# Loads, low parts, softplus and fills moved in a hybrid decoder layer on one core

## The chip, the cores and the metric

The kernel runs on one core of one Trainium2 chip. The core has five engines that the text names by what they are: TensorE (PE in the rows: matmuls; PEld is its weight load), VectorE (DVE), ScalarE (ACT), GpSimd (POOL) and SyncE (SP), which here issues every DMA. The metric is the device time of one execution in microseconds, lower is better. Each engine works through its own list of instructions in order and waits on semaphores for the others.

## The reference

One layer of a Hymba-like decoder over 1040 tokens (16 meta tokens and 1024 of the input) of width 1024. A state-space mixer and a stick-breaking attention read the same projection, their outputs go through one output projection, and a feed-forward block with a short convolution follows.

```python
xn = rms_norm(h, mix_pre_g[l])
proj = xn @ w_in[l]                      # z | x,B,C | dt | q | k | v
...
y_ssd = ssd_mixer(z, xbc, dt_raw, ...)   # conv (4 taps) + silu, softplus(dt), chunked scan, gate with silu(z), norm
y_sb = rms_norm(stick_breaking_attention(q, k, v).reshape(Bsz, L, SB_WIDTH), sb_norm_g[l])
mix = jnp.concatenate([y_ssd, y_sb], axis=-1) @ w_out[l]
h = h + rms_norm(mix, mix_post_g[l])
...                                      # feed-forward: up, conv (3 taps), gelu, gate, down
return h[:, N_META:]
```

In the mixer, chunks of 128 tokens are worked on one after another for two groups of heads; within a chunk `y = y_diag + y_off`, then `y + xs * d_skip`, times `silu(z)`. In the attention, weights are running products of `1 - beta` over the keys.

## The kernel before

Every float32 operand of a matmul is split in a high part (a rounded copy, made by ScalarE) and a low part (the rest, one subtraction on VectorE or GpSimd), and a product takes three matmuls: high by high, high by low, low by high. Names ending in `h`/`hi` and `l`/`lo` are these parts: `wr_B` is a raw weight block, `wh_B` and `wl_B` its parts (`split_hi`, `split_lo`); `whi1z`, `wlo1z`, `wlo4z` and so on are those of weight blocks and of sums of blocks, 128 x 1024 each; `ahz` and `alz` (128 x 512) are the parts of one half of a block, made by `split_22`.

**The head.** The token tiles `xt` are loaded, squared on ScalarE (`square`), scaled with the row weights `gpre` on VectorE (`norm`, tile `xn`), transposed on TensorE (`turn_x`, tile `xtp`) and cut into parts by ScalarE and VectorE. `t1` to `t4` are sums of such tiles for the products below. The code of the head stands in a manual schedule: its instructions run on each engine in the order in which they are written.

**Products.** A `Duo` multiplies a pair of weight blocks with all tokens by seven products (Strassen's form; `product(n)`, line 308 of the matmuls) that go to three groups of PSUM banks `dA`, `dX`, `dY`. After a product VectorE adds its bank to the raw outcome in SBUF (`craw_x<-dXx`, line 320; ScalarE copies two of the seven, line 317), and the next product that uses the bank waits for that. Between the products of one duo the splits and sums of the next one are issued (`n.split_22`, `n.sums`: the sums are lines 285 to 288 on GpSimd), and in seven slots the conv taps (`conv_acts`: four taps on VectorE, lines 505 and 508, on 128 x 1040) and the softplus of dt (`dt_acts`: `loads` with the tiny `fold` and the memset of `dtk`, `turn_dt`, `soft_a`, `soft_b`, `decay`).

**What sets the order there.** From line 614 a schedule holds the order of PE, DVE, ACT and POOL as it is written, up to what the tile framework puts ahead by its own priorities; the lists that result are shown below.

**The scan.** 18 units (two groups by nine chunks). `load_zx` loads the gate `zk` and the skip term `xd`, 128 x 4 x 128 float32 each; `chunk_outputs` makes the scaled carried state `yt` (line 1116); `chunk_store` multiplies the chunk (`yt<-em,xdt`, line 1136), fills with products of q and k (`scan_fill`), adds `yt` by transposes (line 1141), and then VectorE adds `xd` (line 1145, which frees the PSUM bank for the next unit's line 1136) and multiplies by `zk` (line 1146). SyncE's list is part of the order here. The DMAs take eight completion semaphores (DMAHW0 to DMAHW7) in turn, so that a DMA is issued when the one eight places ahead of it has landed.

**The entry of attention.** `hold` is a 128 x 1040 bfloat16 mask for the scans over keys (`pair_weights`, line 1314): zero, with ones in the last 128 columns that an `affine_select` on GpSimd cuts to a triangle. `token_rstd` makes the norm of the mixer's output; its tile `tmsa` has a column that is set to one.

Of the kernel before, what the change touches and what calls it, by code (L numbers as in the profile page):

```python
# [17 lines left out]
P = 128  # L18
# [48 lines left out]
def tile_layer(ctx: ExitStack, tc: tile.TileContext, x, meta, rows, parts,  # L67
# [190 lines left out]
    class Duo:  # L258
# [14 lines left out]
        def split_22(self):  # L273
            h, l = (weight_rows(sa.tile([P, 5 * P], F32R, tag=f"a22{e}", name=f"a{e}{self.nm}", bufs=2), 4, OFF22)
                    for e in "hl")
            raw = self.r[1][:, HI4]
            nc.scalar.activation(h, raw, AF.Copy)
            nc.gpsimd.tensor_tensor(l, raw, h.bitcast(F32), op=ALU.subtract)
            self.w["a22"] = h, l
# [44 lines left out]
    with tc.tile_pool(name="pre", bufs=3, side="right") as pre:  # L324
# [14 lines left out]
        raws = {"B0": raw_of("B0", w_xbc[8])}  # L339
        gpre = row_bcast(pre, 0, D, "gpre")  # L340
        load_x(2)
        load_x(3)
# [83 lines left out]
        split_hi("B0")  # L426
        split_lo("B0")
        square(2)
        root(2)
        norm(2)  # L430
        turn_x(0)
        square(3)
# [192 lines left out]
    def dt_acts():  # L625
# [30 lines left out]
        def soft_a():  # L656
            dtx = box["dtx"]
            e, s, s2 = box["e"], box["s"], box["s2"] = [t3(n) for n in ("e1", "s1", "s2")]
            nc.vector.scalar_tensor_tensor(e, dtx, -1.0, dtx, op0=ALU.mult, op1=ALU.min)
            nc.scalar.activation(e, e, AF.Exp)  # L660
            nc.vector.tensor_scalar(s, e, 2.0, None, op0=ALU.add)
            nc.vector.reciprocal(s, s)
            nc.vector.tensor_tensor(s, s, e, op=ALU.mult)
            nc.vector.tensor_tensor(s2, s, s, op=ALU.mult)
# [42 lines left out]
        return [[loads], [turn_dt], [soft_a], [soft_b], [lambda: decay(0)], [lambda: decay(1)],  # L707
# [39 lines left out]
    for i, q in enumerate(duos):  # L747
# [3 lines left out]
        for j, m in enumerate((1, 5, 2, 6, 7, 3, 4) if i == 0 else (1, 6, 5, 7, 2, 3, 4)):  # L751
            q.product(m)
            if i == 0:
                if m == 1:
                    d0.split_4()
                elif m == 6:
                    split_t(t4l.bitcast(F32), xo["t4"], nc.vector)
            if n is not None:
                if m == 1:
                    n.split_22()  # L760
                elif m == 6:
                    n.sums()
                elif m == 7:
                    n.split_3()
                elif m == 2:
                    n.split_1()
                elif m == 3:
                    n.split_4()
            elif m in (7, 2):
                v_split(1, int(m == 2))  # L770
            for act in slots[j]:
                act()
# [4 lines left out]
        if i == 1:  # L777
            slots = merged(slots, [[], dts[2], [], dts[3], [], [], []]) + [dts[4], dts[5], dts[6]]
# [199 lines left out]
    def token_rstd(r, pool, nm, pt, scalar=False):  # L978
# [6 lines left out]
        (nc.gpsimd if scalar else nc.vector).memset(ms[:, 0:1], 1.0)  # L985
# [14 lines left out]
    with tc.tile_pool(name="ssd", bufs=1, side="right") as sp:  # L1000
# [49 lines left out]
        def load_zx(g, c):  # L1050
            a, b = (M0, NM) if c == 0 else (NM + (c - 1) * P, NM + c * P)
            y0 = M0 if c == 0 else 0
            zx = []
            for t, d in (("zk", zd), ("xd", xdd)):
                zx.append(sp.tile([P, 4, P], F32, tag=t, name=f"{t}{g}_{c}", bufs=3 if t == "zk" else 2))
                nc.sync.dma_start(out=zx[-1][:, :, y0:y0 + b - a], in_=d[g][:, :, a:b].rearrange("b p t -> p b t"))
            zxs[g, c] = zx
# [129 lines left out]
        load_zx(*units[0])  # L1187
# [4 lines left out]
        for n, (g, c) in enumerate(units):  # L1192
# [6 lines left out]
            if n + 3 < len(units):  # L1199
                load_bc(*units[n + 3])  # L1200
            if n < 2:
# [3 lines left out]
            if n + 1 < len(units):  # L1205
                load_zx(*units[n + 1])
# [62 lines left out]
    nc.vector.memset(hold, 0.0)  # L1269
    nc.vector.memset(hold[:, L - P:], 1.0)  # L1270
# [1225 lines left out]
```

## Time and profile before

| | |
|---|---|
| time, median of 3 runs | 1657.96 us (1655.59 to 1659.79) |
| the profiled execution: time | 1657.8 us |
| its span in the trace | 1655.8 us |
| mean granted clock of TensorE | 0.997 of full speed |
| TensorE busy | 1626.7 us, 98% |
| VectorE / ScalarE / GpSimd busy | 1087.5 / 748.1 / 782.1 us |
| DMA queue of SyncE | 244.48 MB, 45.8% of 16 engines |

The rows further down are those of the profiled execution. Its time is longer than its span by 2.0 us, which lie around the span. A time in a row is counted from the start of the span, and an instruction's duration includes what it spends held up after its start.

### The profile page before, as it was taken

The numbers are of one execution on the slowest core, as the hardware profiler recorded it, in microseconds if no ns is written. First come the engines' busy times: TensorE is split into PE (matmuls) and PEld (weight loads), VectorE is DVE, ScalarE is ACT, GpSimd is POOL, SyncE is SP. The second block draws the span as 40 slices with busy tenths as digits, with TensorE's granted clock in tenths as the row PEclk, the third lists the DMA queues.
The fourth block names the chain that finished last, engine by engine and source line by source line (L and its number), as shares of the span: only waits on it lengthen the run. The fifth ranks groups of instructions, "written<-read, shape, count | busy, mean of one in ns | idle before, by whom it ended". The sixth has DMA issues, their size and how long they took to land.

```text
span 1655.8 us, 28995 instructions
## 1 busy us (share of the span) xinstructions
PE 1626.7 (98%) x11508; PEld 1434.1 (87%) x11508; DVE 1087.5 (66%) x1248; ACT 748.1 (45%) x1100; POOL 782.1 (47%) x579
## 2 busy tenths in 40 slices
PE   7999999999999999999999999999999999999998
PEld 6999999978877888888877889999999999888886
DVE  6975744344367599999840677765666556658877
ACT  7454344332234367766741445433333333344544
POOL 2876877520457463454421113777777677200001
PEclk9999999999999999999999999999999999999999
DMA  4544335334588776545254542222333322495345
GB/s 173 185 154 133 104 121 194 135 138 145 148 236 266 212 235 207 155 123 154 60 193 151 165 161 90 96 96 96 98 107 113 108 98 83 142 332 175 96 119 180
DMA packets 164518, 247.39 MB, mean 149 GB/s; under 512 B 18487, under 2 KB 99495, under 8 KB 162702
## 3 DMA queue, kind: packets, MB, share of 16 engines
q1 hardware_dynamic: 163806, 244.48, 45.8%
q8 instruction: 91, 1.49, 0.4%
q10 hardware_dynamic: 576, 1.05, 0.2%
q14 instruction: 45, 0.37, 0.1%
HBM read 161.99 MB, written 83.46 MB: 148 GB/s over the span
## 4 chain that ended last, share of the span: by engine, by line
PE 89%; DVE 5%; issue 2%; POOL 2%; DMA 2%; ACT 1%; POOLq 0%; DVEq 0%; SPq 0%; ACTq 0%
PE fX L1900 10%; PE mo L1504 10%; PE dnA L2312 7%; PE fY L1900 7%; PE fA L1900 7%; PE dnB L2312 5%; PE av L1352 3%; PE tw L1332 3%; PE z L1308 3%; PE pj_q L218 3%; DVE kp L1314 2%; PE pj_k L218 2%; PE dXz L308 2%; PE dXqk L308 2%; PE dXx L308 2%
## 5 line engine op out<-in xcount | busy, mean ns | idle before, releaser
L1314 DVE TENSOR_TENSOR_SCAN kp<-kp,hold 128x396 f32<-128x396 f32 (+5 forms) x224 | 211.2, 1014 | 20.2 <-ACT kp L1309 18.4
L182 POOL TENSOR_TENSOR wlo<-wr,whi 128x1024 fp32r<-128x1024 f32 x43 | 99.3, 2318 | 40.8 <-ACT whi L181 40.8
L2349 POOL TENSOR_TENSOR fms<-fms 128x1 f32<-128x1 f32 x8 | 2.3, 288 | 222.0 <-DMA ar<-fda 185.9
L181 ACT ACTIVATE whi<-wr 128x1024 fp32r<-128x1024 f32 x43 | 45.7, 1063 | 112.2 <-PE fX L1900 76.2
L1972 DVE SCALAR_TENSOR_TENSOR ga<-gr,pp,ga 128x1024 f32<-128x1024 f32 x44 | 69.4, 1577 | 34.1 <-ACT ga L1965 33.3
L2234 ACT ACTIVATE dh<-ar 128x512 fp32r<-128x512 f32 x77 | 48.6, 631 | 94.1 <-PE dnB L2312 44.7
L2235 DVE TENSOR_TENSOR dl<-ar,dh 128x512 fp32r<-128x512 f32 x77 | 53.2, 691 | 47.1 <-ACT dh L2234 47.1
L1309 ACT ACTIVATE kp<-z 128x788 f32<-128x788 f32 (+4 forms) x96 | 72.7, 832 | 16.6 <-PE z L1308 12.4
L1337 ACT ACTIVATE th<-tw 128x1024 f32<-128x1024 f32 (+2 forms) x96 | 70.8, 813 | 15.6 <-PE tw L1332 15.6
L1352 PE MATMUL av<-th,v 128*64 128x128 f32 x1152 | 70.0, 275 | 2.0 <-POOL tmsa L985 0.9
L1332 PE MATMUL tw<-ident,kp 128*128 128x128 f32 x576 | 70.0, 276 | 0.8 <-ACT st L935 0.5
L1332 PEld LDWEIGHTS tw<-ident,kp 128*128 128x128 f32 x576 | 62.4, 141 | 8.0 <-issue 6.5
L1352 PEld LDWEIGHTS av<-th,v 128*64 128x64 f32 x1152 | 62.3, 137 | 8.0 <-issue 3.9
L2312 PE MATMUL dnA<-dl,dh 128*128 128x512 f32 x176 | 68.5, 389 | 0.0
L2312 PE MATMUL dnA<-dh 128*128 128x512 f32 x176 | 68.5, 389 | 0.0
L2312 PE MATMUL dnA<-dh,dl 128*128 128x512 f32 x176 | 68.5, 389 | 0.0
L1286 POOL TENSOR_SCALAR cb<-kp 128x32 f32<-128x32 f32 x64 | 42.9, 678 | 50.5 <-DVE kp L1314 46.9
L2033 POOL TENSOR_TENSOR al<-wr,ah 128x512 fp32r<-128x512 f32 x20 | 28.6, 1430 | 77.6 <-ACT ah L2032 77.5
L1308 PE MATMUL z<-k,q 64*128 64x396 f32 (+9 forms) x672 | 62.3, 329 | 1.0 <-DVE st L941 1.0
L1308 PEld LDWEIGHTS z<-k,q 64*128 64x128 f32 x672 | 53.1, 185 | 10.8 <-ACT th L1337 4.2
L2312 PE MATMUL dnB<-dh 128*128 128x512 f32 x132 | 51.3, 389 | 0.0
L2312 PE MATMUL dnB<-dh,dl 128*128 128x512 f32 x132 | 51.3, 389 | 0.0
(987 smaller groups left out, 6026.4 us busy)
## 6 DMA issues: line engine op xcount, KB each, us to landing
wr<-in_w_up SPq DMA_DIRECT2D x44, 512.0 KB
fds<-ga SPq DMA_DIRECT2D x44, 256.0 KB
b<-in_w_down SPq DMA_DIRECT2D x44, 256.0 KB
ar<-fds SPq DMA_DIRECT2D x44, 256.0 KB
fda<-ga SPq DMA_DIRECT2D x33, 256.0 KB
ar<-fda SPq DMA_DIRECT2D x33, 256.0 KB
k<-qkd SPq DMA_DIRECT2D x8, 1040.0 KB
q<-qkd SPq DMA_DIRECT2D x64, 128.0 KB
```

What stands on the lines that cost most here:

```text
L182: nc.gpsimd.tensor_tensor(l, raw, h.bitcast(F32), op=ALU.subtract)
L218: mm(acc[:, :CQ - s], a[:, k, :], b[:, k % 4, c + s:c + CQ], start=(k == 0 and j == 0), stop=(k == KB - 1 and j == 2))
L308: mm(acc[:, c, :CQ], u[:, k, :], v[:, k, c * CQ:(c + 1) * CQ], start=first and k == 0 and j == 0, stop=k == 3 and j == 2, skip_group_check ...
L1308: mm(z[:, j, a - lo:e - lo], u[h, :], r[h, a - bases[x]:e - bases[x]], start=s_ == 0, stop=s_ == 2)
L1309: nc.scalar.activation(kp[:, :, lo:top], z[:, :, :top - lo], AF.Sigmoid, scale=-QSCALE)
L1314: nc.vector.tensor_tensor_scan(part, part, hold[:, L - last + a:L - last + e][:, ::-1], 1.0 if e == last else kp[:, j, e:e + 1], op0=ALU.m ...
L1332: nc.tensor.transpose(tw[:, j, b, :], kp[:, j, c0:c0 + P], ident)
L1337: copied[0] = nc.scalar.activation(th[:, :, :nb, :], tw[:, :, :nb, :], AF.Copy, scale=-1.0, bias=1.0).ins
L1352: mm(av[halves[j], 1 - x, :], v[:, kb, halves[j]], th[:, j, b, :], start=kb == 0, stop=kb == i)
L1504: recent[0] = mm(acc, u[:, k, :], v[:, cs], start=(k == 0 and j == 0), stop=(k == 7 and j == 2))
L1900: mm(acc[:, c, :nn], u[:, k, :], v[:, k, c0:c0 + nn], start=first and k == 0 and j == 0, stop=k == 3 and j == 2, skip_group_check=not first)
L2312: mm(banks[BANK[n], t], u[:, 0, c], v[:, 1, :], start=(n in (1, 2, 5) and p == 0 and i == 0), stop=(p == NPR - 1 and i == 2), skip_group_c ...
```

## The change

In the head, the load of `gpre` and that of the third token tile go ahead of the load of `wr_B`, and the split of `wr_B` goes behind the third tile's square (high part) and the first tile's transposes (low part). The first duo's successor gets its `alz` on VectorE instead of GpSimd. The middle of the softplus becomes a step of its own (`soft_m`), one slot later, and its last part moves with it. In the scan, `load_zx` loads `xd` first and `zk` second, and the unit's state loads and pending stores are issued between the two. At the entry of attention the two fills of `hold` go from VectorE to GpSimd, and the column of `tmsa` is a ScalarE copy instead of a GpSimd memset.

```diff
@@ -270,12 +270,12 @@
         def split_1(self):
             self.w["a11"], self.w["a12"] = split_w(self.r[0], f"1{self.nm}")
 
-        def split_22(self):
+        def split_22(self, eng=nc.gpsimd):
             h, l = (weight_rows(sa.tile([P, 5 * P], F32R, tag=f"a22{e}", name=f"a{e}{self.nm}", bufs=2), 4, OFF22)
                     for e in "hl")
             raw = self.r[1][:, HI4]
             nc.scalar.activation(h, raw, AF.Copy)
-            nc.gpsimd.tensor_tensor(l, raw, h.bitcast(F32), op=ALU.subtract)
+            eng.tensor_tensor(l, raw, h.bitcast(F32), op=ALU.subtract)
             self.w["a22"] = h, l
 
         def sums(self):
@@ -336,9 +336,9 @@
 
         load_x(0)
         load_x(1)
-        raws = {"B0": raw_of("B0", w_xbc[8])}
         gpre = row_bcast(pre, 0, D, "gpre")
         load_x(2)
+        raws = {"B0": raw_of("B0", w_xbc[8])}
         load_x(3)
         raw_dt = pre.tile([P, KB, 16], F32, tag="wdt", name="wr_dt", bufs=1)
         nc.sync.dma_start(out=raw_dt, in_=w_dt)
@@ -423,12 +423,12 @@
             root(i)
         norm(0)
         norm(1)
-        split_hi("B0")
-        split_lo("B0")
         square(2)
         root(2)
         norm(2)
+        split_hi("B0")
         turn_x(0)
+        split_lo("B0")
         square(3)
         root(3)
         norm(3)
@@ -658,6 +658,9 @@
             e, s, s2 = box["e"], box["s"], box["s2"] = [t3(n) for n in ("e1", "s1", "s2")]
             nc.vector.scalar_tensor_tensor(e, dtx, -1.0, dtx, op0=ALU.mult, op1=ALU.min)
             nc.scalar.activation(e, e, AF.Exp)
+
+        def soft_m():
+            e, s, s2 = box["e"], box["s"], box["s2"]
             nc.vector.tensor_scalar(s, e, 2.0, None, op0=ALU.add)
             nc.vector.reciprocal(s, s)
             nc.vector.tensor_tensor(s, s, e, op=ALU.mult)
@@ -704,7 +707,7 @@
         def store():
             nc.sync.dma_start(out=dtkd, in_=dtk)
 
-        return [[loads], [turn_dt], [soft_a], [soft_b], [lambda: decay(0)], [lambda: decay(1)],
+        return [[loads], [turn_dt], [soft_a], [soft_m], [soft_b], [lambda: decay(0)], [lambda: decay(1)],
                 [lambda: decay(2), store, turn_acs]]
 
     v_stack = ExitStack()
@@ -757,7 +760,7 @@
                     split_t(t4l.bitcast(F32), xo["t4"], nc.vector)
             if n is not None:
                 if m == 1:
-                    n.split_22()
+                    n.split_22(nc.gpsimd if i else nc.vector)
                 elif m == 6:
                     n.sums()
                 elif m == 7:
@@ -775,7 +778,7 @@
         for k, acts_ in enumerate(extra):
             slots[k] = acts_ + slots[k]
         if i == 1:
-            slots = merged(slots, [[], dts[2], [], dts[3], [], [], []]) + [dts[4], dts[5], dts[6]]
+            slots = merged(slots, [[], dts[2], dts[3], [], dts[4], [], []]) + [dts[5], dts[6], dts[7]]
         if i == n_early:
             t_stack.close()
             vl = v_stack.enter_context(tc.tile_pool(name="vl", bufs=1, side="left"))
@@ -982,7 +985,10 @@
             a, nr = (M0, 2) if t == 0 else (NM + (t - 1) * P, P)
             mm(pt[:nr, t:t + 1], sq[:, a:a + nr], ones[:, 0:1], start=True, stop=True)
         ms = pool.tile([P, NT + 1], F32, tag="tms", name=f"tms{nm}")
-        (nc.gpsimd if scalar else nc.vector).memset(ms[:, 0:1], 1.0)
+        if scalar:
+            nc.scalar.activation(ms[:, 0:1], ones[:, 0:1], AF.Copy)
+        else:
+            nc.vector.memset(ms[:, 0:1], 1.0)
         for rows_, cols_ in ((slice(0, 2), slice(0, 1)), (slice(0, P), slice(1, NT + 1))):
             if scalar:
                 nc.scalar.activation(ms[rows_, cols_], pt[rows_, cols_], AF.Copy, scale=1.0 / D, bias=EPS)
@@ -1051,9 +1057,10 @@
             a, b = (M0, NM) if c == 0 else (NM + (c - 1) * P, NM + c * P)
             y0 = M0 if c == 0 else 0
             zx = []
-            for t, d in (("zk", zd), ("xd", xdd)):
-                zx.append(sp.tile([P, 4, P], F32, tag=t, name=f"{t}{g}_{c}", bufs=3 if t == "zk" else 2))
-                nc.sync.dma_start(out=zx[-1][:, :, y0:y0 + b - a], in_=d[g][:, :, a:b].rearrange("b p t -> p b t"))
+            for t, d in (("xd", xdd), ("zk", zd)):
+                zx.insert(0, sp.tile([P, 4, P], F32, tag=t, name=f"{t}{g}_{c}", bufs=3 if t == "zk" else 2))
+                nc.sync.dma_start(out=zx[0][:, :, y0:y0 + b - a], in_=d[g][:, :, a:b].rearrange("b p t -> p b t"))
+                yield
             zxs[g, c] = zx
 
         def chunk_weights(g, c):
@@ -1184,7 +1191,7 @@
         put_stores()
         set_rows(2)
         load_bc(*units[2])
-        load_zx(*units[0])
+        run(load_zx(*units[0]), 3)
         cur = chunk_weights(*units[0])
         chunk_mask(*units[0], *cur)
         run(fill, 16 - FIRST)
@@ -1198,12 +1205,13 @@
                 load_x(*units[n + 2])
             if n + 3 < len(units):
                 load_bc(*units[n + 3])
+            zx_steps = load_zx(*units[n + 1]) if n + 1 < len(units) else iter(())
+            run(zx_steps, 1)
             if n < 2:
                 put_stores()
             if n in (0, 2, 6, 10):
                 load_state(n // 2 + 2, n // 2 + (4 if n else 3))
-            if n + 1 < len(units):
-                load_zx(*units[n + 1])
+            run(zx_steps, 2)
             nxt = chunk_weights(*units[n + 1]) if n + 1 < len(units) else None
             yt, zk, xd, prev[g] = chunk_outputs(g, c, *cur)
             if nxt:
@@ -1266,8 +1274,8 @@
     ap = apool.enter_context(tc.tile_pool(name="attn", bufs=1, side="right"))
 
     hold = ap.tile([P, L], BF16, name="hold", tag="hold")
-    nc.vector.memset(hold, 0.0)
-    nc.vector.memset(hold[:, L - P:], 1.0)
+    nc.gpsimd.memset(hold, 0.0)
+    nc.gpsimd.memset(hold[:, L - P:], 1.0)
     nc.gpsimd.affine_select(out=hold[:, L - P:], in_=hold[:, L - P:], compare_op=ALU.is_ge, fill=0.0, base=0,
                             pattern=[[1, P]], channel_multiplier=-1)
```

VectorE's list from the low part of `t2` on, in the stretch of the first duo's products (`cdB` are the conv taps, `dYx` and `dXx` PSUM banks of the duo), before:

```order
L255 TENSOR_TENSOR t2l<-t2r,t2h 128x2080
L505 TENSOR_SCALAR cdB_851<-craw_B_256,pp 128x1040
L508 SCALAR_TENSOR_TENSOR cdB_851<-craw_B_256,pp,cdB_851 128x1040
L636 TENSOR_TENSOR fold<-ident 32x16
L255 TENSOR_TENSOR t3l<-t3r,t3h 128x2080
L320 TENSOR_TENSOR craw_x_838<-dYx_867,craw_x_838 128x520
L508 SCALAR_TENSOR_TENSOR cdB_851<-craw_B_256,pp,cdB_851 128x1040 x2
L320 TENSOR_TENSOR craw_x_840<-dXx_926,craw_x_838 128x520
```

And of the change:

```order
L255 TENSOR_TENSOR t2l<-t2r,t2h 128x2080
L255 TENSOR_TENSOR t3l<-t3r,t3h 128x2080
L278 TENSOR_TENSOR alz_848<-wrz_802,ahz_847 128x4x128
L505 TENSOR_SCALAR cdB_851<-craw_B_256,pp 128x1040
L508 SCALAR_TENSOR_TENSOR cdB_851<-craw_B_256,pp,cdB_851 128x1040
L636 TENSOR_TENSOR fold<-ident 32x16
L320 TENSOR_TENSOR craw_x_838<-dYx_867,craw_x_838 128x520
L508 SCALAR_TENSOR_TENSOR cdB_851<-craw_B_256,pp,cdB_851 128x1040 x2
L320 TENSOR_TENSOR craw_x_840<-dXx_926,craw_x_838 128x520
```

`t3l` moved ahead of the first two taps and `alz` came in behind it; `fold`, the evacuations of `dYx` and `dXx` and the last two taps stand behind all of them.

SyncE's list in the scan, from a table load (`sg`) to the loads of the fourth unit's `zk` and `xd` (`bt`, `ct`, `bn` are state loads), with what each waits for, before:

```order
L1040 DMA sg_4472<-diagd_808 8x1024 [waits DMAHW3_49]
L1014 DMA bt_4461<-bcd_596 128x256 [waits DMAHW4_49]
L1015 DMA ct_4462<-bcd_597 128x256 [waits DMAHW5_49]
L1018 DMA bn_4463<-bnd_600 128x256 [waits DMAHW6_49]
L1014 DMA bt_4464<-bcd_598 128x256 [waits DMAHW7_49]
L1015 DMA ct_4465<-bcd_599 128x256 [waits DMAHW0_49]
L1018 DMA bn_4466<-bnd_601 128x256 [waits DMAHW1_49]
L1056 DMA zk_1_4847<-zd_114 128x4x128 [waits DMAHW2_49,Activation_49]
L1056 DMA xd_1_4849<-xdd_102 128x4x128 [waits DMAHW3_49,DVE_49]
```

And of the change:

```order
L1046 DMA sg_4472<-diagd_808 8x1024 [waits DMAHW3_49]
L1062 DMA xd_1_4841<-xdd_102 128x4x128 [waits DMAHW4_49,DVE_49]
L1020 DMA bt_4461<-bcd_596 128x256 [waits DMAHW5_49]
L1021 DMA ct_4462<-bcd_597 128x256 [waits DMAHW6_49]
L1024 DMA bn_4463<-bnd_600 128x256 [waits DMAHW7_49]
L1020 DMA bt_4464<-bcd_598 128x256 [waits DMAHW0_49]
L1021 DMA ct_4465<-bcd_599 128x256 [waits DMAHW1_49]
L1024 DMA bn_4466<-bnd_601 128x256 [waits DMAHW2_49]
L1062 DMA zk_1_4849<-zd_114 128x4x128 [waits DMAHW3_49,Activation_49]
```

`xd` moved from behind the six state loads and `zk` to the place ahead of them; `zk` stands where `xd` stood. Both wait for a semaphore of a landing eight places earlier.

## Rows read from the trace of the kernel before

**Rows 1.** TensorE's waits: tile waited with <- tile waited for: us, times, longest.
```profile
PE xtp L383 <- DVE xn L369: 12.1, 5, 10.2
...
PE av L1352 <- POOL tmsa L985: 0.9, 1, 0.9
```

**Rows 2.** Timeline of TensorE: start, us, instruction, [idle before <- releaser].
```profile
69.23 0.39 PE L308 MATMUL dXx<-t3h,whi3x 128*128 128x260 f32 x1 [0.96 <-DVE craw_x L320]
...
85.52 0.58 PE L308 MATMUL dXz<-t2h,wlo4z 128*128 128x260 f32 x1 [1.05 <-POOL wlo4z L182]
...
467.61 1.85 PE L1136 MATMUL yt<-em,xdt 128*64 128x128 f32 x16 [2.02 <-DVE xd L1145]
...
471.74 0.60 PE L1141 MATMUL yt<-ident,yt 128*128 128x128 f32 x4
```

**Rows 3.** Stretches: us; busy PE, PEld, DVE, ACT, POOL; PEclk, DMA share, GB/s.
```profile
69.40:72.40 3.00, 3.00 (x26) 2.98 (x27) 0.86 (x1) 2.11 (x2) 2.92 (x3) 1.00 1.03 399
85.50:88.80 3.30, 3.28 (x15) 3.28 (x16) 2.85 (x2) 0.53 (x2) 2.62 (x2) 0.50 0.77 308
467.80:471.10 3.30, 3.30 (x24) 2.97 (x22) 2.11 (x5) 0.63 (x1) 2.77 (x3) 0.50 0.90 272
```

**Rows 4.** Timeline of VectorE in the head.
```profile
8.83 2.47 DVE L369 SCALAR_TENSOR_TENSOR xn<-xt,rs_pre,gpre 16x1024 f32<-16x1024 f32 x2 [6.71 <-DMA gpre<-in_rows]
```

**Rows 5.** Timeline of ScalarE in the head.
```profile
7.18 1.06 ACT L415 ACTIVATE wh_B<-wr_B 128x1024 fp32r<-128x1024 f32 x1
...
21.60 0.38 ACT L249 ACTIVATE sq<-pj_dt 32x260 f32<-32x260 f32 x1 [0.41 <-PE pj_dt L247]
...
23.47 0.57 ACT L393 ACTIVATE b11h<-xtp 128x480 fp32r<-128x480 f32 x1 [0.45 <-PE xtp L383]
...
58.91 1.95 ACT L254 ACTIVATE t3h<-t3r 128x2080 fp32r<-128x2080 f32 x1 [3.35 <-DVE t2l L255]
...
65.35 1.06 ACT L181 ACTIVATE whi1z<-wrz 128x1024 fp32r<-128x1024 f32 x1
```

**Rows 6.** Timeline of VectorE around the first products.
```profile
58.80 0.81 DVE L505 TENSOR_SCALAR cdB<-craw_B,pp 128x1040 f32<-128x1040 f32 x1
59.65 1.30 DVE L508 SCALAR_TENSOR_TENSOR cdB<-craw_B,pp,cdB 128x1040 f32<-128x1040 f32 x1
...
60.95 2.31 DVE L255 TENSOR_TENSOR t3l<-t3r,t3h 128x2080 fp32r<-128x2080 f32 x1
...
63.79 4.77 DVE L508 SCALAR_TENSOR_TENSOR cdB<-craw_B,pp,cdB 128x1040 f32<-128x1040 f32 x2
68.49 0.69 DVE L320 TENSOR_TENSOR craw_x<-dXx,craw_x 128x520 f32<-128x520 f32 x1
```

**Rows 7.** Timeline of GpSimd in the same stretch.
```profile
62.65 2.67 POOL L182 TENSOR_TENSOR wlo4x<-s24x,whi4x 128x1024 fp32r<-128x1024 f32 x1 [5.95 <-ACT whi4x L181]
65.27 2.19 POOL L278 TENSOR_TENSOR alz<-wrz,ahz 128x512 fp32r<-128x512 f32 x1
67.41 0.70 POOL L637 MEMSET dtk<- 128x720 f32 x1
68.07 2.56 POOL L182 TENSOR_TENSOR wlo1z<-wrz,whi1z 128x1024 fp32r<-128x1024 f32 x1
...
82.29 3.18 POOL L182 TENSOR_TENSOR wlo4z<-s24z,whi4z 128x1024 fp32r<-128x1024 f32 x1
```

**Rows 8.** Timeline of SyncE in the scan (DMA issues).
```profile
456.57 0.35 SPq L1014 DMA_DIRECT2D bt<-bcd  x1
...
460.88 0.45 SPq L1056 DMA_DIRECT2D xd<-xdd  x1
```

**Rows 9.** Timeline of VectorE in the scan.
```profile
466.78 0.69 DVE L1145 TENSOR_TENSOR xd<-yt,xd 128x512 f32<-128x512 f32 x1 [5.77 <-DMA xd<-xdd]
```

**Rows 10.** Timeline of GpSimd at the entry of attention.
```profile
593.53 0.09 POOL L985 MEMSET tmsa<- 128x1 f32 x1
```

**Rows 11.** Timeline of VectorE at the entry of attention.
```profile
579.25 13.81 DVE L1314 TENSOR_TENSOR_SCAN kp<-kp,hold 128x396 f32<-128x396 f32 x14 [1.78 <-POOL hold L1271]
```

## The prediction

> **What bounds the kernel now.** The first section of the page gives TensorE 98% of the span, so time can be won or lost only where TensorE waits or runs slower. I read three views in turn. The waits of TensorE name what it stood for, in total [rows 1]: 12.1 us for the first normalized tiles `xn` (10.2 of them before its first instruction) and 0.9 for `tmsa`. TensorE's timeline shows three more [rows 2]: 0.96 us for `craw_x`, 1.05 for `wlo4z`, 2.02 in the scan for the `xd` addition. All five places are touched by the change. The table of stretches then shows what a wait can cost behind it [rows 3]: after the `wlo4z` wait and after the `xd` wait the granted clock is 0.50 for 3.3 us with TensorE busy throughout. That is the 1.2 GHz level instead of 2.4, so each stretch does half its work and costs about 1.7 us. After the 0.96 us it stayed at 1.00. Last, the timelines of the other engines give the durations. The order of TensorE's own instructions is the same in both kernels, so every term below is a wait of TensorE or a slow stretch.
>
> **a. Loads in the head: -0.75 us (-0.9 to 0).** The first `xn` waits for `gpre` until 8.83 [rows 4]; the first use of `wr_B` is at 7.18 [rows 5], so the 512 KB load of `wr_B` ahead of `gpre` puts `gpre` at most 1.6 us back, and `gpre` now takes its place. But ScalarE copies without a break behind 11.1 and shows only two waits before the head's end, 0.41 and 0.45 us [rows 5]. Those, 0.86, are what an earlier `xn` can give; I take 0.75, since `x3` is not moved forward.
>
> **b. `t3l` and `alz` ahead of the taps: +5.3 us (+2.9 to +6.6).** This term is seen in the order and not in the diff: VectorE now does `t3l`, `alz`, two taps and `fold` before it comes to the other two taps and to `craw_x<-dXx`, for which TensorE already waits 0.96 us. `t3l` cannot start before its `t3h` ends on ScalarE at 60.86 [rows 5], as it did before (60.95). So 3.4 us of work that stood ahead of `t3l` or on GpSimd now stands behind it. To that come GpSimd's turns: two taps, 1.30 each alone, take 4.77 while `wlo4x` ends and `alz` runs [rows 6, 7], so the two engines' instructions add up here. Step by step, from `wlo4x`'s end at 65.3 [rows 7], which stays: `alz` on VectorE, 0.6 (512 columns at the rate of `t3l`'s 2.31 for 2080), 65.9. First tap 0.81, second 1.30: 68.0. By then `whi1z` is there (65.35 + 1.06, [rows 5]), so `wlo1z` gets its turn; of the 2.56 in its row 0.45 lies behind a tap, so 2.1: 70.1. (`fold` and the evacuation of `dYx` go beside it.) Third tap: 71.4. The first of GpSimd's sums, half as many elements as `wlo1z`: 1.05, 72.5. Fourth tap: 73.8. `craw_x<-dXx`, 0.69: 74.5, against 69.2 now. That is +5.3. If GpSimd gets nothing in behind `wlo4x`, the evacuation of `dYx` (0.69, as its like in [rows 6]) is exposed instead and the end is 72.1: +2.9. If one more of GpSimd's sums gets in, with what it holds up some 1.3: +6.6. A gain is excluded, since even without any turn of GpSimd `alz`, two taps and `fold` have come behind `t3l`.
>
> **c. The clock behind that wait: +1.7 us (0 to 1.7).** A wait of 1.05 us was followed by 3.3 us at 0.50, one of 0.96 was not [rows 2, 3]. A wait of 6 us is nearer to the first; I take the full price.
>
> **d. The `wlo4z` wait goes: -2.7 us.** TensorE comes to `wlo4z` at 84.47 and gets it at 85.5 [rows 2, 7]. After a delay of 5.3 (or of 2.9) it comes at 89.8 (87.4), past that end. So the 1.05 us and the slow stretch behind, 1.7, are not paid a second time. The three together: 5.3 + 1.7 - 2.7 = +4.3 us (2.9 + 0 - 2.7 = +0.2, to 6.6 + 1.7 - 2.7 = +5.6). The tap chain also feeds ScalarE's silu and stores, for which TensorE waits in no row.
>
> **Softplus: nothing.** Its middle and last parts each move by one product or less. TensorE waits for none of it in the views, and products cover it; without the cover it would cost less than the chain's own few small instructions, under 1 us, which I leave in the range.
>
> **e. `xd` ahead of `zk`: -3.2 us (-3.7 to 0).** One unit of the scan waits, the fourth. Its `xd` is issued at 460.88, behind six loads and `zk`, the first of which went at 456.57 [rows 8], and the addition waits until 466.78 [rows 9], 5.9 us after the issue. In the new order `xd` takes the place at 456.57 and lands near 462.5, before TensorE comes to the next `yt` at 465.6. So 2.0 + 1.7 = 3.7 us go. `zk`, however, now stands where `xd` stood: issued about 460.9, landing 466.8. On VectorE the product with `zk` stands behind the addition, and behind that one small copy and the scaling of `yt`, which TensorE's transposes need: 466.8 + 0.7 + 0.3 + 0.7 = 468.5. TensorE gets there at 465.6 + 1.1 for `yt` + 1.4 for the twelve products between them, which took 2.3 at the half clock [rows 2]: 468.1. So about 0.45 is paid again. No other unit's addition holds TensorE in the trace, so there a place in the queue costs nothing.
>
> **f. Entry of attention: -0.7 us (-0.9 to +0.1).** `tmsa`'s memset stands on GpSimd at 593.53 [rows 10], and `av` waits 0.9 for it [rows 1]. On ScalarE it is one tiny copy ahead of its user. The `hold` memsets go to GpSimd, which clears 720 columns in 0.70 [rows 7], so 1040 in 1.0; VectorE's first scan already waits 1.78 us for `hold` [rows 11] and will start later by 0 to 1.0. I take +0.2 for it.
>
> **Sum.** -0.75 + 4.3 + 0 - 3.2 - 0.7 = -0.35 us on the profiled execution's 1657.8 us (span 1655.8 and 2.0 around it): 1657.45. The median of the runs is 0.16 above that execution, so 1657.6. Three places gain, one loses, and the two sides are about as large.
>
> **A rule that speaks against the change.** I let `fold`, 32x16, go beside `wlo1z`, since no row shows an instruction so small held back. If it is held like the taps [rows 6, 7], the evacuation of `dYx` behind it is late too and another sum gets in: the +6.6 end of b instead of 5.3, and the sum +0.95. The Trainium skill says this, on the page "SBUF — State Buffer", section "Who interferes with whom": a VectorE instruction with two SBUF inputs contends with a GpSimd instruction that reads SBUF, and the later one blocks until the first has ended. By that rule the trace agrees for the taps, 4.77 instead of 2.6 us; for `fold` no run here shows it.
>
> **The rivals.** The forecast, chance 0.55: the pieces cancel, 1657.6; alone 1655.5 to 1659.
> A, 0.27: GpSimd is not in the way behind `wlo4x` and no slow stretch follows, so b to d come to +0.2. For it speaks that GpSimd's turns hang on tenths of a microsecond; against it the 4.77 us of two taps. -0.75 + 0.2 - 3.2 - 0.7 = -4.45: 1653.5. With every gain at its end (-0.9 + 0.2 - 3.7 - 0.9 = -5.3): 1652.7.
> B, 0.10, the slower side: the scan's wait only changes its name, `zk` for `xd`. With the same wait e is 0: 1660.8. It makes the kernel slower by over 0.3% when e becomes +2.1, a wait of 4.1 us and its slow 1.7 against the 3.7 saved; for that `zk` must land 9.5 us after its issue, instead of the 5.9 of `xd`. Six loads stand ahead of it, but small ones.
> C, 0.08: `fold` is held, as worked out above: 1658.9.
>
> **How the numbers follow.** 0.3% of the time is 5.0 us, about what a measurement of this kernel can tell from no change: faster is below 1653.0, slower above 1662.9. Faster: the lower part of A (0.12) and the low edge of the forecast (0.03), 0.15. Slower: half of B (0.05) and the upper edges of the forecast and of C (0.04), 0.09. Same: 0.76. The range for 8 in 10 goes from A's middle part, 1653.0, to the upper end of b (+1.3) with e at 0 (+3.2), 1662.0.
>
> **What would show it.** Right: a wait of TensorE of 5 to 7 us for `craw_x` that ends near 74, a stretch at clock 0.50 behind it, no `wlo4z` wait, no `xd` wait at 465 and at most half a microsecond at the transposes, no `tmsa` wait. Wrong: `craw_x<-dXx` ending before 72, or a clock of 1.00 behind the wait (A); a wait of 2 us or more behind `zk` (B); a wait in attention for `hold` that was not there.

## The result and the profile after

The changed kernel takes 1660.64 us, median of 18 runs (1658.12 to 1665.1); the kernel before took 1657.99 in as many runs beside it (1655.06 to 1661.01). The ratio is 1.0019 with a 95% interval from 1.0012 to 1.0026, which is some 3 us, 2.0 to 4.3. The time lies in the range that was given, and the change is less than 0.3%; but the small difference has the other sign: forecast -0.4, measured +2.6.

TensorE's waits in the profiled execution after (tile waited with <- tile waited for: us, times, longest), against [rows 1, 2]:

```profile
PE xtp L383 <- DVE xn L369: 11.0, 5, 8.5
PE dXx L308 <- DVE craw_x L320: 7.4, 1, 7.4
...
PE pz L685 <- DVE s L678: 0.7, 1, 0.7
```

The waits for `wlo4z`, `xd` and `tmsa` are gone from the list and the first wait has become shorter, 11.0 instead of 12.1. In their place stands one wait of 7.4 us for `craw_x`, and a small new one for the softplus tile `s`. TensorE's timeline at the same instructions as in [rows 2], with the block of dt products (18 small ones in a row) and the first `pz` besides:

```profile
74.98 0.59 PE L308 MATMUL dXx<-t3h,whi3x 128*128 128x260 f32 x1 [7.41 <-DVE craw_x L320]
...
89.24 2.09 PE L649 MATMUL tpd<-fold,sq 32*16 32x16 f32 x18
...
91.61 0.28 PE L308 MATMUL dXz<-t2h,wlo4z 128*128 128x260 f32 x1
...
136.05 0.21 PE L685 MATMUL pz<-s,tri 16*16 16x16 f32 x2 [0.71 <-DVE s L678]
...
472.54 1.10 PE L1143 MATMUL yt<-em,xdt 128*64 128x128 f32 x16
...
475.11 0.60 PE L1148 MATMUL yt<-ident,yt 128*128 128x128 f32 x4
```

Since TensorE's list is the same in both kernels, the difference of the start of one instruction is the sum of all that lies ahead of it. At the wait for `craw_x` TensorE came at 74.98 - 7.41 = 67.57, before at 69.23 - 0.96 = 68.27: 0.7 ahead. Behind it the instruction started at 74.98 instead of 69.23, 5.75 late. At `wlo4z` it is 91.61 to 85.52, 6.1. At `yt` in the scan 472.54 to 467.61, 4.9, at the transposes 475.11 to 471.74, 3.4. At the last matmul the trace has +2.5, near the +2.65 of the medians, but that nearness is in part luck. The spans differ by 3.5 (1659.3 and 1655.8), because 1.0 more lies behind the last matmul here; that tail is 6.45 to 7.5 us, counted from the last matmul's start, in the executions of this case, also of kernels whose code there is the same. So most of the loss lies between 68 and 75, and the largest gain comes in the scan, where it was expected. The table of stretches shows the clock (PEclk is the third number from the right):

```profile
74.90:78.30 3.40, 3.32 (x15) 3.32 (x16) 1.04 (x2) 2.35 (x2) 1.84 (x2) 0.50 0.18 17
88.00:91.20 3.20, 3.20 (x30) 3.03 (x28) 1.40 (x3) 2.40 (x4) 0.00 (x0) 1.00 0.15 62
92.40:95.20 2.80, 2.80 (x15) 2.80 (x14) 2.76 (x2) 0.00 (x0) 2.64 (x3) 0.50 0.33 129
473.20:476.60 3.40, 3.40 (x31) 3.09 (x28) 2.76 (x7) 1.93 (x3) 2.37 (x3) 1.00 0.89 270
```

Behind the wait the clock is 0.50 until 78.3, as expected. It is 0.50 again from 92.4 to 95.2, where there was no wait at all: from 88.0 to 91.2 TensorE is busy throughout at 1.00, and what it did last there is the block of 18 products of dt, 32 x 16 each. In the kernel before the same block stands ahead of the slow stretch at 85.5, and the `wlo4z` wait of [rows 2] follows it:

```profile
81.95 2.09 PE L649 MATMUL tpd<-fold,sq 32*16 32x16 f32 x18
```

In the scan the clock stays at 1.00. VectorE and GpSimd around the wait, against [rows 6, 7]:

```profile
60.23 2.33 DVE L255 TENSOR_TENSOR t3l<-t3r,t3h 128x2080 fp32r<-128x2080 f32 x1 [2.01 <-ACT t3h L254]
62.47 2.68 DVE L278 TENSOR_TENSOR alz<-wrz,ahz 128x512 fp32r<-128x512 f32 x1
...
65.93 3.20 DVE L508 SCALAR_TENSOR_TENSOR cdB<-craw_B,pp,cdB 128x1040 f32<-128x1040 f32 x1
69.05 1.23 DVE L636 TENSOR_TENSOR fold<-ident 32x16 f32<-32x16 f32 x1
...
70.81 3.50 DVE L508 SCALAR_TENSOR_TENSOR cdB<-craw_B,pp,cdB 128x1040 f32<-128x1040 f32 x2
74.24 0.69 DVE L320 TENSOR_TENSOR craw_x<-dXx,craw_x 128x520 f32<-128x520 f32 x1
```

```profile
61.99 2.62 POOL L182 TENSOR_TENSOR wlo4x<-s24x,whi4x 128x1024 fp32r<-128x1024 f32 x1 [5.95 <-ACT whi4x L181]
64.55 0.70 POOL L637 MEMSET dtk<- 128x720 f32 x1
65.83 2.19 POOL L182 TENSOR_TENSOR wlo1z<-wrz,whi1z 128x1024 fp32r<-128x1024 f32 x1 [0.59 <-ACT whi1z L181]
67.99 2.26 POOL L285 TENSOR_TENSOR wrz<-wrz 128x512 f32<-128x512 f32 x1
70.33 2.89 POOL L286 TENSOR_TENSOR wrz<-wrz,wrz 128x512 f32<-128x512 f32 x1
```

Read the two lists together. `alz` takes 2.68 us instead of the 0.6 of its size: it is held until `wlo4x` ends at 64.6. The second tap takes 3.20 instead of 1.30 and is held until `wlo1z` ends at 68.0. `fold` takes 1.23 instead of 0.16 and is held until L285 ends at 70.25. The last two taps take 3.50 instead of 2.6, with L286 between them. GpSimd has an instruction ready at each gap, and three of its turns fit behind `wlo4x`.

In the scan, VectorE at the fourth unit:

```profile
467.71 0.69 DVE L1152 TENSOR_TENSOR xd<-yt,xd 128x512 f32<-128x512 f32 x1 [0.35 <-PE yt L1148]
472.68 0.69 DVE L1153 TENSOR_TENSOR zk<-xd,zk 128x512 f32<-128x512 f32 x1 [4.28 <-DMA zk<-zd]
...
473.62 0.68 DVE L1123 TENSOR_TENSOR yt<-yf,dtk 128x512 f32<-128x512 f32 x1
```

`xd`'s addition now waits 0.35 us for TensorE and not for a load. The product with `zk` waits 4.28 us for its load and holds the scaling of `yt` until 474.3; TensorE's transposes come at 475.1 and do not notice. At the entry of attention, VectorE:

```profile
582.37 18.19 DVE L1322 TENSOR_TENSOR_SCAN kp<-kp,hold 128x396 f32<-128x396 f32 x18 [2.26 <-POOL hold L1279]
```

GpSimd's first fill takes 0.97 us, and the first scan waits 2.26 us for `hold` instead of 1.78 [rows 11]. It starts 3.1 us later than before, where TensorE is 3.4 late, since VectorE has no fills of its own ahead of it now. TensorE shows no wait for `hold`.

In the head, TensorE's first instruction starts at 8.52 instead of 10.16. Of ScalarE's two waits in [rows 5] the 0.41 is gone; the other stands as it was:

```profile
22.82 0.57 ACT L393 ACTIVATE b11h<-xtp 128x480 fp32r<-128x480 f32 x1 [0.45 <-PE xtp L383]
```

### The profile page after: what moved, and what is told of

It is laid out like the page before. It is cut to its first block, busy times and chain, and to the rows that moved or that the text cites. A ratio compares the mean times of both kernels' runs of the same rounds, so it can differ in the third digit from the quotient of the medians.

```text
span 1659.3 us, 28998 instructions
## 1 busy us (share of the span) xinstructions
PE 1626.9 (98%) x11508; PEld 1434.7 (86%) x11508; DVE 1091.2 (66%) x1247; ACT 748.5 (45%) x1101; POOL 778.3 (47%) x579
## 3 DMA queue, kind: packets, MB, share of 16 engines
q10 hardware_dynamic: 576, 1.05, 0.2%
## 4 chain that ended last, share of the span: by engine, by line
PE 61%; DVE 2%; issue 1%; ACT 1%; DVEq 0%; POOLq 0%; ACTq 0%; POOL 0%
PE fX L1908 10%; PE mo L1512 10%; PE dnA L2320 7%; PE fY L1908 7%; PE fA L1908 7%; PE dnB L2320 5%; PE av L1360 3%; PE tw L1340 3%; PE z L1316 2%; DVE kp L1322 2%; PE g0a L1922 1%; PE x2tp L1786 0%; PE pj_q L218 0%; PE pj_k L218 0%; PE g0d L1922 0%
```

## The experiments

Each one's ratio is against the kernel before on the same chip, and 0.001 of it is 1.7 us.

**One part alone: `alz` on VectorE (e1)** (line 278 and its call, nothing else).

```diff
-                    n.split_22()
+                    n.split_22(nc.gpsimd if i else nc.vector)
```

> The kernel before with one part alone: alz on VectorE, which also puts t3l ahead of the taps. Theory 1 (fold is held up and the slow stretch behind the wlo4z wait belongs to the dt transposes ahead of it): the wait for craw_x 7.4 us as in the changed kernel, 6.4 more than before, 1.7 of slow clock behind it, 1.0 back at wlo4z, so +7.1 us against the kernel before. Theory 2 (the forecast's step: fold goes free, the slow stretch goes with the wlo4z wait): a wait of 6.3, no slow stretch near 92, +4.3 us. Rival: the wait comes from the head's moved loads and not from alz; then the wait stays at 1.0 and the time at +0.

1662.18 us, ratio 1.0035 (1.0021 to 1.0049): +5.8. TensorE's wait, then the stretch near 92:

```profile
PE dXx L308 <- DVE craw_x L320: 7.4, 1, 7.4
```

```profile
92.00:96.00 4.00, 4.00 (x36) 4.00 (x35) 3.96 (x4) 0.00 (x0) 3.84 (x3) 1.00 0.31 120
```

The wait of 7.4 comes from this part alone, so the head's loads have no share in it. The stretch near 92 stayed at 1.00 here, as theory 2 had it. But this is the same block of small products as in the changed kernel, where it fell; one execution does not decide that point. The size lies between the two expectations, and its interval, 3.5 to 8.1 us, takes in both.

This run also shows how far executions differ in the head, which e1, e10 and e11 have unchanged. The same TensorE instruction behind it, in the kernel before and then in e1:

```profile
61.68 0.39 PE L308 MATMUL dAx<-b21h,whi1x 128*128 128x260 f32 x1 [0.64 <-ACT craw_x L317]
60.20 0.40 PE L308 MATMUL dAx<-b21h,whi1x 128*128 128x260 f32 x1 [0.65 <-ACT craw_x L317]
```

e10 comes to it at 60.74, e11 at 60.26, and the changed kernel at 61.01. The four products `pj_dt<-b11h` ahead of it take 1.22 us before and 0.72 in e1: TensorE's speed goes up earlier in one execution than in the other.

**The softplus put back (e2)** in the changed kernel (the diff shows one of three places; the function `soft_m` and the slots go back with it).

```diff
-        return [[loads], [turn_dt], [soft_a], [soft_m], [soft_b], ...
+        return [[loads], [turn_dt], [soft_a], [soft_b], ...
```

> The changed kernel with the softplus steps where they were before. Theory 1 (the moved step makes TensorE wait for s at pz): that wait of 0.7 us (0.9 to 1.1 with the pause behind it) near 135 goes, -1.0 us against the changed kernel, so +1.6 to +2.0 against before. Theory 2 (the wait comes from the 7 us by which everything is late in the changed kernel, since VectorE has more to do behind it): the wait stays, 0 against the changed kernel.

1661.67 us, ratio 1.0027 (1.0015 to 1.0038): no gain. Of TensorE's waits the 7.4 us stayed and this is new:

```profile
PE dYx L308 <- DVE craw_x L320: 1.4, 1, 1.4
```

The wait at `pz` went, and one of 1.4 us for `craw_x` at `dYx` came. VectorE there:

```profile
125.08 2.18 DVE L664 TENSOR_TENSOR s<-s 128x144 f32<-128x144 f32 x1
```

The last product of the softplus's middle takes 2.18 us, since GpSimd's `wlo3z` (124.83 to 127.09) has its turn; the evacuation stands behind it, at 127.18. In the kernel before the same instruction takes 0.31 us, from 118.44: there `wlo3z` started at 118.92, 0.2 us after it was done. In the changed kernel the middle stands behind that evacuation, takes 2.20 there, and `pz` pays for it. Both theories missed that: it is again a turn of GpSimd, and which instruction it holds depends on tenths of a microsecond.

**`fold` on GpSimd (e3)** in the changed kernel.

```diff
-            nc.vector.tensor_tensor(fold, ident[:32, 0:16], ident[:32, 16:32], op=ALU.add)
+            nc.gpsimd.tensor_tensor(fold, ident[:32, 0:16], ident[:32, 16:32], op=ALU.add)
```

> The changed kernel with the tiny fold made on GpSimd. Theory 1 (fold, held for 1.1 us, delays the evacuation of dYx, the last two taps and craw_x): the wait for craw_x falls from 7.4 to 6.3, -1.1 us against the changed kernel. Theory 2 (GpSimd's sums get in at some other gap anyway, so that the sum of the two engines' work decides): the wait stays within 0.3 of 7.4.

1660.1 us, ratio 1.0017 (1.0009 to 1.0026); the wait is 7.1. VectorE, then GpSimd:

```profile
65.82 3.09 DVE L508 SCALAR_TENSOR_TENSOR cdB<-craw_B,pp,cdB 128x1040 f32<-128x1040 f32 x1
...
69.44 3.91 DVE L508 SCALAR_TENSOR_TENSOR cdB<-craw_B,pp,cdB 128x1040 f32<-128x1040 f32 x2
```

```profile
63.93 0.66 POOL L636 TENSOR_TENSOR fold<-ident 32x16 f32<-32x16 f32 x1
...
65.20 2.61 POOL L182 TENSOR_TENSOR wlo1z<-wrz,whi1z 128x1024 fp32r<-128x1024 f32 x1
67.77 2.26 POOL L285 TENSOR_TENSOR wrz<-wrz 128x512 f32<-128x512 f32 x1
70.11 2.14 POOL L286 TENSOR_TENSOR wrz<-wrz,wrz 128x512 f32<-128x512 f32 x1
```

Theory 2 held: without `fold` on VectorE the last two taps take 3.91 instead of 3.50, and L286 still gets its turn ahead of the evacuation, which starts at 73.28. So the one small instruction does not decide. That both engines' work adds up over the whole stretch is how the rows read; no run takes an instruction of GpSimd out of the stretch to test it alone.

**`alz` on VectorE, but behind the evacuation of `dXx` (e4).**

```diff
             nc.scalar.activation(h, raw, AF.Copy)
-            eng.tensor_tensor(l, raw, h.bitcast(F32), op=ALU.subtract)
+            self.low = lambda: eng.tensor_tensor(l, raw, h.bitcast(F32), op=ALU.subtract)
+            if eng is not nc.vector:
+                self.low()
...
                 elif m == 6:
+                    n.low()
                     split_t(t4l.bitcast(F32), xo["t4"], nc.vector)
```

> The changed kernel with alz still on VectorE, but issued behind the evacuation of dXx; t3l then stands behind the first two taps again, as before. Theory 1 (the place of t3l and alz ahead of the taps is the loss, not alz on VectorE): the wait for craw_x is 1 us or less, no slow stretch behind it, no wlo4z wait either since GpSimd has 2.2 us less to do; against the changed kernel -6.4 - 1.7 = -8, so about -5 against before. Theory 2 (any alz on VectorE costs what it saves on GpSimd): a wait of 2 us or more for craw_x or for a later evacuation, and a time within 2 us of before.

1654.24 us, ratio 0.9982 (0.9973 to 0.999): -3.0 against before and 6 below the changed kernel. `t3l` is back behind two taps and `fold`. VectorE, then GpSimd:

```profile
63.06 5.98 DVE L510 SCALAR_TENSOR_TENSOR cdB<-craw_B,pp,cdB 128x1040 f32<-128x1040 f32 x2
68.96 0.69 DVE L322 TENSOR_TENSOR craw_x<-dXx,craw_x 128x520 f32<-128x520 f32 x1
69.57 0.68 DVE L279 TENSOR_TENSOR alz<-wrz,ahz 128x512 fp32r<-128x512 f32 x1
```

```profile
65.76 2.19 POOL L182 TENSOR_TENSOR wlo1z<-wrz,whi1z 128x1024 fp32r<-128x1024 f32 x1 [0.54 <-ACT whi1z L181]
70.33 1.30 POOL L287 TENSOR_TENSOR wrz<-wrz 128x512 f32<-128x512 f32 x1 [2.38 <-DVE alz L279]
```

`alz` takes 0.68 with GpSimd idle. The wait for `craw_x` is 2.2, not 1: `wlo1z`, which found `alz` ahead of it on GpSimd before, now gets its turn between the last two taps (5.98 instead of 4.77). So moving `alz` away does not free that stretch, it lets the next one in. No `wlo4z` wait is left. The time is between the two theories: the loss is gone, as theory 1 had it, and a wait of 2 us stays, as theory 2 had it.

**Four corners for the slow stretch near 85 (e5 to e8).** All four have the head, the scan and the entry of the change, and the softplus of before; then `alz` on GpSimd (with its `wlo4z` wait) or late on VectorE (without), and the 18 products of dt in one block or in three places (`dts[-1]` makes a part of them):

```diff
-             c0_taps[2:4] + b0_turns[1:2], c0_taps[4:] + b0_turns[2:], dts[1]]
+             c0_taps[2:4] + b0_turns[1:2] + [lambda: dts[-1](0, 3)], c0_taps[4:] + b0_turns[2:] + [lambda: dts[-1](3, 6)], dts[1]]
```

> The kernel before with three parts: the head's loads, the scan's order, the entry of attention; alz and softplus as before. The terms of the forecast, as the trace of the changed kernel has them, for these parts: -0.7 - 3.4 - 0.9 = -5.0 us against before. The waits for craw_x (about 1.0) and wlo4z (about 1.0) stay, and so does the slow stretch near 85. Theory 1 (the stretch belongs to the 18 small products of dt) and theory 2 (it belongs to the wlo4z wait) say the same here; it is one corner of four. Rival: the head's gain is used up by later waits, then -4.3.

> The kernel of e5 with the 18 small products of dt given out in three places of six, between the big products, with the wlo4z wait as it is. Theory 1 (the block of small products brings the slow stretch): no stretch at 0.50 near 85, -1.7 us against e5. Theory 2 (the wait of 1 us brings it): the stretch stays, 0 against e5.

> The kernel of e5 with alz on VectorE behind the evacuation of dXx: no wlo4z wait, the small products in one block. Theory 1: the stretch near 85 stays; against e5 -1.0 for the wait and +1.2 for the longer wait at craw_x (2.2 in e4 instead of 1.0), 0 in sum. Theory 2: no stretch, -1.7 against e5.

> The kernel of e7 with the small products of dt in three places: neither the wlo4z wait nor the block. Theory 1: no stretch near 85, -1.7 against e7 and against e5. Theory 2: no stretch either, 0 against e7.

| kernel | us, median | ratio (95%) |
|---|---|---|
| `alz` on GpSimd, block (e5) | 1654.01 | 0.9976 (0.9964 to 0.9987) |
| `alz` on GpSimd, three places (e6) | 1654.11 | 0.998 (0.9971 to 0.9988) |
| `alz` late, block (e7) | 1655.99 | 0.9994 (0.9984 to 1.0004) |
| `alz` late, three places (e8) | 1656.95 | 0.9999 (0.9988 to 1.0009) |

The stretches of e5, e6 and e7, in this order:

```profile
86.00:89.00 3.00, 3.00 (x17) 3.00 (x16) 1.94 (x1) 0.00 (x0) 2.92 (x2) 0.52 0.53 211
590.60:594.00 3.40, 3.40 (x26) 2.92 (x27) 3.40 (x5) 2.27 (x5) 3.32 (x4) 0.61 1.13 321
```

```profile
85.00:89.00 4.00, 4.00 (x34) 3.97 (x35) 3.25 (x5) 1.07 (x2) 2.86 (x3) 1.00 0.65 262
```

```profile
70.80:73.60 2.80, 2.80 (x15) 2.73 (x15) 2.17 (x1) 0.79 (x2) 2.72 (x3) 0.50 0.33 132
84.00:89.00 5.00, 5.00 (x43) 4.97 (x43) 4.25 (x8) 2.57 (x4) 1.49 (x1) 1.00 0.45 184
```

Against the kernel before, e5 is 3.2 us ahead by the medians (2.2 to 6.0 by the interval), where 5.0 was expected; its profiled execution is the slowest of its twelve. In three places the small products were followed by a clock of 1.00 in e6, and in e8 too; in one block by 0.52 in e5. But e7 has the block and stays at 1.00 near 85, after it fell behind its 2.2 us wait near 70. And the corner with the wait and without the block is empty: in e6 TensorE was late enough for the `wlo4z` wait to vanish. The time shows no gain of the 1.7 us either: the pieces in e6 bring a wait of 0.7 us of their own. e8 has a wait of 3.0 us for `craw_x` at `dYx` and a stretch at 0.50 behind that. It came out slower than e4, from which it differs in the softplus too, but their intervals just touch. e7 came out 2.0 above e5, where 0 or -1.7 was expected. So by their times the four corners decide for neither theory. In e5 a second slow stretch stands at the entry of attention, 0.61 from 590.6 on.

**The change without `alz` (e9), the scan alone (e10), the entry alone (e11), and `alz` one place ahead (e12).** The first three are parts of the diff of the change: all but `split_22` and its call, the three places around `load_zx`, and the fills of `hold` with the column of `tmsa`. The last is the kernel of e4 with the call behind the slot of the third product, so that `alz` stands between the last two taps and the evacuation.

```diff
-                    n.low()
                     split_t(t4l.bitcast(F32), xo["t4"], nc.vector)
...
             for act in slots[j]:
                 act()
+            if i == 0 and m == 2:
+                n.low()
```

> The changed kernel with alz on GpSimd again (the other four parts stay). Theory 1 (alz ahead of the taps is the only loss of the change): against the changed kernel -6.4 - 1.7 + 1.0 = -7.1 in the trace, so -4 to -5 us against before, with the wait for craw_x at 1.0 and the wlo4z wait back. Theory 2 (the moved softplus loses too, 1 us at pz): -3 to -4 against before, and a wait for s at pz of 0.7. Against e5, which is the same without the softplus move: -1.3 if the move takes away the wait for craw_x at dYx that e2, e5 and e8 show, +1 if it brings the wait at pz.

> The kernel before with the scan's part alone. The forecast's step: -3.2 us (no wait for xd, no slow stretch behind it, at most 0.5 us at the transposes). Rival (zk takes over the wait): a wait of 2 us or more behind zk, 0 against before.

> The kernel before with the entry of attention alone. The forecast's step: -0.7 us, the wait for tmsa gone (0.9), hold's fills cost 0.2. Rival (hold's fills on GpSimd delay the first scans and TensorE with them): a new wait in the first 20 us of attention, +0.5 or more. A slow stretch behind the entry, as e5 and e7 show near 591, would hide either by 1.6.

> The kernel of e4 with alz one place further ahead: behind the last two taps and ahead of the evacuation of dXx, so t3l and the taps stand as before and alz alone comes in. Theory 1 (it is the place of t3l that costs, alz is 0.7): the wait for craw_x grows from 2.2 by 0.7 to 2.9. Theory 2 (each VectorE instruction with two inputs in SBUF brings a turn of GpSimd with it): by 0.7 and a turn held of 1.3 to 2.2, so to 4.2 or more. Either way less than the 7.4 of the changed kernel.

Without `alz`: 1655.0 us, ratio 0.9985 (0.9975 to 0.9996), -2.5 us. That is 5.6 below the changed kernel's median on another chip, less than the 7.1 of theory 1. Its waits:

```profile
PE sg L1077 <- DMA sg<-diagd: 1.7, 1, 1.7
PE dXz L308 <- POOL wlo4z L182: 1.0, 1, 1.0
```

The wait for `craw_x` is back at 1.0. The wait at `pz` is not there, so theory 2's extra loss is not either. A wait of 1.7 us for a load of `sg` and a slow stretch from 589.2 to 592.6 took part of the gain in this execution. Against e5 the intervals overlap: the softplus move neither gains nor loses anything that these runs can tell.

The scan alone: 1656.33 us, ratio 0.9987 (0.9977 to 0.9997), -2.2 with 0.5 to 3.8. The forecast's -3.2 is in the interval. Its waits:

```profile
PE av L1354 <- POOL tmsa L985: 1.4, 1, 1.4
```

No wait for `xd`, and 0.2 at the transposes (`yt` at L1142), as before the change; `av` now waits 1.4 for `tmsa` instead of 0.9, so half a microsecond is given back there. The entry alone: 1657.11 us, ratio 0.9995 (0.9986 to 1.0005). -0.7 and nothing can't be told apart by this; the wait for `tmsa` is gone and there is none for `hold`. The `wlo4z` wait is there as in the kernel before, and this execution shows when the clock falls beside it:

```profile
80.54 2.09 PE L649 MATMUL tpd<-fold,sq 32*16 32x16 f32 x18
...
84.09 0.58 PE L308 MATMUL dXz<-t2h,wlo4z 128*128 128x260 f32 x1 [1.02 <-POOL wlo4z L182]
```

```profile
82.60:83.00 0.40, 0.40 (x3) 0.26 (x2) 0.31 (x4) 0.40 (x1) 0.40 (x1) 1.00 0.86 338
83.00:84.10 1.10, 0.08 (x2) 0.01 (x1) 1.10 (x2) 1.10 (x4) 1.03 (x1) 0.50 0.65 262
```

The wait begins at 84.09 - 1.02 = 83.07. The clock is 0.50 from 83.0 on, with TensorE busy until then, so here the wait did not bring the fall.

`alz` one place ahead: 1654.76 us, ratio 0.9988 (0.9978 to 0.9998). The wait:

```profile
PE dXx L310 <- DVE craw_x L322: 2.8, 1, 2.8
```

It grew from 2.2 to 2.8, by the 0.6 of `alz` alone: theory 1. Of the 7.4 us, then, 2.2 are there as soon as `alz` is off GpSimd (1.0 of them were there before), 0.6 are its own time, and the other 4.6 come with `t3l` and `alz` standing ahead of the first two taps. No run separates these two.

## Why the prediction was right or wrong

**Two steps failed, both to the slow side: b counted one turn of GpSimd too few (+1.1), and d took back a slow stretch that stayed (+1.4).** In the profiled execution the softplus came to 1.1 where the sum had nothing. Together these are 3.6 us; the other terms came out 0.55 better, and so the -0.35 of the sum became +2.7. With terms of up to 5.3 us that cancelled to 0.35, each of these misses was enough to turn the sign. That the time still lies in the range is due to the range's width of 9 us.

**b.** The forecast gave GpSimd two turns behind `wlo4x` (`wlo1z` and the first sum) and reached an end of 74.5 on the clock of before, +5.3. There were three, L286 between the taps too, and the end came at 74.93 with the head 0.7 ahead, which is 75.6: +6.4. That is the upper end of the range, which the forecast gave to rival C by holding `fold`. `fold` was held, 1.23 us until L285's end, so C's mechanism is in the trace. The Trainium skill (page "SBUF — State Buffer", section "Who interferes with whom") states that a VectorE instruction with two SBUF inputs contends with a GpSimd instruction that reads SBUF. By that rule the trace agrees, for one as small as 32x16. But e3 takes `fold` away and the wait falls only from 7.4 to 7.1, so `fold` is where one of the turns fell and not the cause. That the cause is the sum of both engines' work fits all the rows shown, e3's and e4's too. The "3.4 us of work" that the forecast put behind `t3l` is 2.9 by its own rows (0.6, 0.81, 1.30 and 0.16); the sum does not use it.

**c was right**: 0.50 behind the wait, +1.6 from 5.75 to 7.3 late.

**d was half right.** The `wlo4z` wait went, 1.05 us. The 1.7 for its slow stretch did not come back: the stretch stood at 92.4 without a wait ahead of it. The sentence "a wait of 1.05 us was followed by 3.3 us at 0.50" joined two things that only stand side by side: TensorE had also just done the block of dt products, which no row of the forecast shows. d was -1.3 instead of -2.7 (from 7.3 to 6.0 late). The stretch is not of one execution: the mean granted clock of the changed kernel's 18 runs is 0.9956, that of the kernel before 0.9964 to 0.9970 beside the experiments, and one stretch of 3.4 us at 0.50 lowers it by 0.0010. Of the profiled executions with the block, nine fell behind it and three did not (e1, e7, e12); the two with the block in pieces did not. Four of the nine (the changed kernel, e2, e3, e4) have no `wlo4z` wait, and in e11 the fall came as the wait began. So the wait is not needed for it. That the block is what brings it is likely but not settled.

**The softplus: the reason failed, the price is not shown.** "TensorE waits for none of it" was wrong in this execution, by 1.1 us (6.0 to 7.1 late at `pz`): the turn of GpSimd in the softplus's middle, which the view of before could not show because it fell just behind there. But e2 puts the softplus back and gains nothing, and e9 is not told apart from e5. The `pz` wait is not steady: e3, e4, e9 and e12 have the same step and no such wait. Nor is the wait that takes its place, 1.3 to 3.0 us at `dYx` in e2, e5, e8 and e11: the kernel before, e1, e6, e7 and e10 have the softplus as before too, and no such wait.

**e was right in mechanism and size**, -3.5 for -3.2 (6.9 late ahead of the scan, 3.4 behind the fourth unit; the 0.45 at the transposes was not paid, as TensorE came at 475.1 and `yt` was ready at 474.3). **f too**, -0.9 for -0.7: the 0.2 for `hold` was not paid.

**a is not shown.** The pair of traces has -0.7 for -0.75. But e1, e10 and e11, with the head of before, are 0.9 to 1.5 ahead of the kernel before at the same instruction near 61, and of the two ScalarE waits that were to give the gain one is still there (two more, 0.46 and 0.37 for VectorE, the forecast did not list; they are there in both kernels). The first products do start earlier, at 8.4 to 9.1 in the ten kernels with the new head and at 9.6 to 10.2 in the four without; how much of that reaches the end no run tells.

Rival A did not occur, and B not either: `zk` does take over the wait on VectorE (4.28 us), but nothing there is wanted before it lands. The terms as this pair of traces has them sum to -0.7 + 6.4 + 1.6 - 1.3 + 1.1 - 3.5 - 0.9 = +2.7, beside +2.5 at the last matmul and +2.6 in the runs.

## What to carry to other kernels

Two engines that take turns have one common budget over a stretch: add the work of both between the fixed start and the instruction that TensorE wants, and take as many turns as the other engine has instructions ready, not as many as the shortest gap suggests. An instruction that is moved to another engine can reorder that engine's list well beyond itself; the cheap version (`alz` behind the wanted evacuation, e4) and the dear one differ by 6 us with the same work on the same engine. Of the parts, the head's loads, the scan's order and the entry together (e5) gave 1654.01, faster than both kernels; `alz` and the softplus were not needed.

## What the hardware showed that was not expected

TensorE's clock can fall with no wait of TensorE just ahead of it, as at 92.4 in the changed kernel or at 83.0 in e11; and it need not fall behind one, as behind the 2.2 us of e4, where e7 fell behind the same wait. Stretches at 0.50 of some 3.4 us also come and go at the entry of attention (e1, e2, e5, e6, e7, e9 and e12 have one there, the kernel before and the changed one not). The times of one kernel differ with it: of e5's twelve, the one of 1650.23 us has a mean clock of 0.999 and the one of 1658.31 has 0.997. The Trainium skill, page "TensorE: Matmul & The Clock Gate", section "What's actually happening", says that the gate watches the engine's recent activity in a window that runs free, so that one kernel can meet it at different points in different runs. The coming and going of the stretches agrees with that. No run here shows the window itself. So a term of 1.7 us read from one execution's slow stretch is a chance, not a price.
